# Two transformer blocks on one core: transposed scalar rows made by a round trip through DRAM instead of by TensorE, and two raw weight tiles given up for four more slabs

## The chip, the core and the metric

The kernel runs on one core of a Trainium2 chip. The metric is the device time of one execution in microseconds, the median of several runs. The engines have separate, in-order instruction queues: TensorE (PE, with its weight loads shown as PEld), VectorE (DVE), ScalarE (ACT), GpSimd (POOL) and SyncE (SP, which here issues nearly all DMAs). An instruction that waits holds up everything behind it on its own engine.

## The reference

Input is a sequence of 256 tokens of width 2048. The first block adds, in turn, a mixer, a cross-attention over 256 memory rows and a convolutional feed-forward network; the second block is a hybrid of two attentions. The two places that matter here are these.

In the gated delta rule (8 heads of width 128, chunks of 64) the running sum of the gates makes a matrix of decays for each head:

```
g = jnp.cumsum(g, axis=-1)
decay = jnp.exp(jnp.where(causal, g[..., :, None] - g[..., None, :], -jnp.inf))
a_strict = jnp.where(strict, jnp.einsum('bhncd,bhnmd->bhncm', k_beta, k) * decay, 0.0)
attn = jnp.einsum('bhncd,bhnmd->bhncm', q, k) * decay
```

In the forgetting attention of the second block (8 heads) a running sum over tokens is added to the logits as a bias:

```
c = jnp.cumsum(log_f, axis=1).transpose(0, 2, 1)
logits = jnp.einsum('bhqd,bhsd->bhqs', qb, k, ...) * scale
return logits + cq[:, :, :, None] - c[:, :, None, :]
```

Both need the same small table (128 tokens on partitions by 16 columns: two halves of the sequence, eight heads) in two forms: as a column, one value for each partition, and as a row, the 128 values of one column repeated on all partitions.

## The kernel before, in words

Everything is fp32, computed as products of a high and a low part. All weights are streamed as 704 units of 128 rows by up to 1024 columns (512 KB). For each unit SyncE loads a raw tile (`load`, L365), ScalarE casts it to the high part `whi` (`split_hi`, L372), VectorE subtracts to get the low part `wlo` (`split_lo`, L382) and, as soon as that subtraction is queued, the next load is queued that will reuse this raw tile (`self.load(i + self.NRAW)`: with 8 raw tiles, the load of the unit eight further on). TensorE then multiplies high by high and low (L227), low by high (L231) and for the last block of a job once more (L244). ScalarE is three units ahead of TensorE and VectorE two.

All other work is written as Python generators. `stream` issues one unit, then lets each live generator go to its next `yield`. So a `yield` puts off the rest of a generator by one unit of the stream, about 2.8 us, and the order on each engine is fixed when the program is built.

Intermediate tiles of 128 x 512 floats (2 KB for each partition) come from `S()`, a pool of 55 "slabs"; a new tile takes the slab of a tile that is done, and its first write waits for the last read of that one. A raw tile takes as much as two slabs.

Three stages are touched or spoken of:

- The gates, p_ba (about 40 to 110 us). The running sums land in PSUM and are copied to the table `G` (shown as `keep`, L651). For each of four groups of four heads, `spread` turns four columns to rows: VectorE multiplies a matrix of ones by a column (`dg`, L453, four instructions), TensorE transposes each (L460), and VectorE subtracts the column and takes the negative magnitude (`E`, L665 and L667). The decays are first used at L722.
- The triangular solve, `X`, `Y`, `L` (L765 to L822), runs in four passes from about 170 to 400 us. In a pass, an inverted 16 x 16 base goes out to DRAM (`dA`, `dX`) and back (`X<-dX`, L778). TensorE transposes X into PSUM (L786), ScalarE copies that to `Y` (L789), TensorE multiplies by Y (L797). At the same time `g_mem` (L985 to L1012) reads the memory rows (`mr`) and ScalarE writes their high parts into new slabs (`x`, L1006). `x1` to `x16` are the sixteen tiles of the normalised input, read by the first projections until about 372 us.
- The forgetting attention, fox (about 1860 to 1970 us): `spread` turns two columns for each head, and `fb` (L1385) is the bias.

Of the kernel before, what the change touches and what calls it, by code (L numbers as in the profile page):

```python
# [9 lines left out]
F32 = mybir.dt.float32  # L10
# [6 lines left out]
MUL, ADD, SUB, MAXI, MINI = ALU.mult, ALU.add, ALU.subtract, ALU.max, ALU.min  # L17

P = 128
TOK = 256  # L20
# [79 lines left out]
def r3(ap, n):  # L100
    return ap.rearrange("p (a b) -> p a b", a=n)


def bc(col, n):
    return col.unsqueeze(2).to_broadcast([P, col.shape[1], n])
# [15 lines left out]
class Builder:  # L121
    LOOK_HI = 3
    LOOK_LO = 2
    NRAW = 8

    def __init__(self, ctx, tc, A):
        self.tc, self.nc, self.A = tc, tc.nc, A
# [16 lines left out]
        return pool.tile([P, w], dt, tag=tag, bufs=bufs, name=f"{nm}{self.n}")  # L144

    def S(self, nm, dt=F32):
        return self._t(self.sp, 512, "s", 55, nm, dt)

    def H(self, nm):
        return self._t(self.sp, TOK, "h", 18, nm, F32)  # L150
# [298 lines left out]
    def spread(self, cols, n):  # L449
# [10 lines left out]
            self.T.transpose(ps[:, i * P : (i + 1) * P], w[:, i * P : (i + 1) * P], self.ident)  # L460
        return ps

    def g_rms(self, R, acc, width):

        ps = yield from self.sums([acc])
        yield
        v = self.Cc("v")[:, 0:2]
        self.V.tensor_scalar(v, ps[:, 0:2], 1.0 / width, EPS, MUL, ADD)
        self.psdone()
        R.c = yield from self.rsq(v, 2)  # L470
        ps = yield from self.spread(R.c, 2)
        yield
        R.b = self.H("rb")
        self.AC.copy(R.b, ps[:, 0:TOK])  # L474
        self.psdone()
        R.ok = True
# [134 lines left out]
    def p_ba(self, ps):  # L611
        V, AC = self.V, self.AC
        r = self.H("ba")
        yield from self.times(ps, r, self.r_mix)
        yield
        yield
        while self.psfree < 1:
            yield
        q = self.ps()
        for t in range(2):  # L620
            self.T.transpose(q[:, t * P : (t + 1) * P], r[:, t * P : (t + 1) * P], self.ident)
        yield
        b, z = self.Cc("b"), self.Cc("z")
        b3, z3, q3 = r3(b, 2), r3(z, 2), r3(q[:, 0:TOK], 2)
        V.tensor_copy(b3, q3[:, :, 0:8])
        V.tensor_tensor(z3, q3[:, :, 32:40], bcm(self.col("dtb", 0, 8), 2), ADD)
        self.psdone()
        n, m = self.Cc("n"), self.Cc("m")
        V.scalar_tensor_tensor(n, b, -1.0, b, MUL, MINI)
        V.tensor_scalar(m, b, 0.0, None, MINI)  # L630
        AC.activation(n, n, AF.Exp)
        AC.activation(m, m, AF.Exp)
        ea = self.Cc("ea")[:, 0:8]
        AC.activation(ea, self.col("alog", 0, 8), AF.Exp)
        sp = yield from self.softplus(z, 16)
        V.tensor_scalar(n, n, 1.0, None, ADD)
        V.reciprocal(n, n)
        self.beta = self.gb
        V.tensor_tensor(self.beta, n, m, MUL)
        g = self.Cc("g")  # L640
        V.scalar_tensor_tensor(r3(g, 2), r3(sp, 2), -1.0, bcm(ea, 2), MUL, MUL)
        yield
        yield
        while self.psfree < 1:
            yield
        q = self.ps()
        self.T.matmul(q[:, 0:16], self.upper, g, start=True, stop=True)
        self.T.matmul(q[:, 16:32], self.ones, g, start=True, stop=True)
        yield
        G = self.gG  # L650
        V.tensor_copy(G, q[:, 0:16])  # L651
        ed = self.Cc("ed")
        V.tensor_tensor(ed, q[:, 16:32], G, SUB)
        self.psdone()
        V.tensor_scalar(ed, ed, 0.0, None, MINI)
        AC.activation(self.gE, G, AF.Exp)
        AC.activation(self.gD, ed, AF.Exp)
        self.dec = {}
        for g in range(2):
            for t in range(2):  # L660
                c = G[:, t * 8 + g * 4 : t * 8 + g * 4 + 4]
                q = yield from self.spread(c, 4)
                yield
                e = self.S("E")
                V.tensor_tensor(r3(e, 4), r3(q, 4), bc(c, P), SUB)  # L665
                self.psdone()
                V.scalar_tensor_tensor(e, e, -1.0, e, MUL, MINI)  # L667
                self.dec[g, t] = e
        for e in self.dec.values():
            AC.activation(e, e, AF.Exp)  # L670
        self.gates.ok = True
# [653 lines left out]
    def p_rf(self, ps):  # L1325

        V = self.V
        r = self.H("rf")
        yield from self.times(ps, r, self.rr)
        yield  # L1330
        yield
        while self.psfree < 1:
            yield
        q = self.ps()
        for t in range(2):
            self.T.transpose(q[:, t * P : (t + 1) * P], r[:, t * P : (t + 1) * P], self.ident)
        yield from self.rope(r, self.kr, [self.kr[0:64]])
        self.nc.sync.dma_start(self.kr[64:128], self.kr[0:64])
        self.kr_ev.ok = True
        z = self.Cc("fz")  # L1340
        V.tensor_tensor(r3(z, 2), r3(q[:, 0:TOK], 2)[:, :, 64:72], bcm(self.col("bf", 0, 8), 2), ADD)
        self.psdone()
        V.tensor_scalar(z, z, -1.0, None, MUL)
        sp = yield from self.softplus(z, 16)
        lf = self.Cc("lf")
        V.tensor_scalar(lf, sp, -1.0, None, MUL)
        yield
        while self.psfree < 1:
            yield
        q = self.ps()  # L1350
        self.T.matmul(q[:, 0:8], self.upper, lf[:, 0:8], start=True, stop=True)
        self.T.matmul(q[:, 8:16], self.upper, lf[:, 8:16], start=True, stop=False)
        self.T.matmul(q[:, 8:16], self.ones, lf[:, 0:8], start=False, stop=True)
        yield
        V.tensor_copy(self.cum, q[:, 0:16])
        self.psdone()
        self.cum_ev.ok = True

    def p_qrope(self, j):
# [13 lines left out]
    def g_head(self, score, vals, hcol, out, i, mla):  # L1373
        V, AC, T = self.V, self.AC, self.T
        spans = ((0, 0, P), (1, P, 3 * P))
        bias = None
        if not mla:
            while not (self.cum_ev.ok and self.rr.ok):
                yield
            cols = self.Cc("ck")[:, 0:2]  # L1380
            V.tensor_copy(cols, r3(self.cum, 2)[:, :, i])
            ps = yield from self.spread(cols, 2)
            yield
            bias = self.S("fb")
            V.scalar_tensor_tensor(bias[:, 0:P], ps[:, 0:P], cols[:, 0:1], self.neg[:, 0:P], SUB, ADD)  # L1385
            V.scalar_tensor_tensor(bias[:, P : 3 * P], ps[:, 0:TOK], cols[:, 1:2], self.neg[:, P:], SUB, ADD)
            self.psdone()
        bias = self.neg if bias is None else bias
        while not score.ready():
            yield  # L1390
# [2 lines left out]
        ps = self.ps()  # L1393
# [19 lines left out]
        ps = self.ps()  # L1413
# [9 lines left out]
        ps = self.ps()  # L1423
        c = slice((i % 4) * P, (i % 4 + 1) * P)
# [99 lines left out]
    def build(self):  # L1524
# [54 lines left out]
        first = [mi(32, self.p_ba)] + self.order(gd, zz, sc)  # L1579
        first = self.skew(first, 3, False)  # L1580
# [62 lines left out]
        for si, (a, b) in enumerate(SECTIONS):  # L1643
# [25 lines left out]
            d = self.skew(down, 4)  # L1669
# [64 lines left out]
        gates = [pj(11 + n if n < 8 else 27 + n, self.p_outgate(n)) for n in range(16)]  # L1734

        def fox():
            hs = [self.g_head(self.fox_score(h), self.fvv, 8 + h, self.oat, h, False) for h in range(8)]
            self.add(self.g_chain(hs[0::2]))
            self.add(self.g_chain(hs[1::2]))
# [155 lines left out]
```

## Time and profile before

| | us |
|---|---|
| median of 3 runs | 2075.57 |
| lowest and highest | 2075.34, 2075.96 |
| the profiled execution, device time | 2078.43 |
| span in its trace | 2076.6 |
| TensorE busy in the span | 2054.0 (99%) |
| VectorE, ScalarE, GpSimd busy | 1480.2 (71%), 1088.6 (52%), 158.6 (8%) |

The profiled execution is 2.86 us above the median of the runs; 1.83 us of it lie outside the span. Matmuls are pipelined and their modelled ends overlap the next one's start, so a time from start to start says what one costs on TensorE.

### The profile page before, as it was taken

The page shows a single profiled execution, that of the slowest core. Times are in us where ns is not written, and L with a number is a line of the kernel's source. Part 1 is how long each engine was busy: PE and PEld are TensorE (multiplying, and loading weights), DVE is VectorE, ACT ScalarE, POOL GpSimd, SP SyncE. Part 2 cuts the span into 40 slices and gives each one's busy share as a digit, 9 for nine tenths or more (in the row PEclk, how much of TensorE's full clock was granted, in tenths as well). Part 3 has the DMA queues.
Part 4 walks back from the last instruction along what each step waited for, and adds up shares of the span by engine and source line. Part 5 has one row for each costly group of instructions (what it writes and reads, how often), then busy time and mean ns, then how long its engine had stood idle before and what let it go on. Part 6 is the DMA issues. An engine that isn't in the chain of part 4 may idle for free.

```text
span 2076.6 us, 31002 instructions
## 1 busy us (share of the span) xinstructions
PE 2054.0 (99%) x11730; PEld 1802.1 (87%) x11730; DVE 1480.2 (71%) x2384; ACT 1088.6 (52%) x1736; POOL 158.6 (8%) x149
## 2 busy tenths in 40 slices
PE   9999999899999999999999999999999999999998
PEld 7888898788888898888888888888888888888886
DVE  7988679565467667777875777756879877656755
ACT  6665555444445555455543455434556655445653
POOL 1020011000001001100000000000009420000000
PEclk9999999999999999999999999999999999999999
DMA  8455446446565535556555656555555669544552
GB/s 302 161 184 185 159 155 196 142 152 193 193 223 185 173 119 182 190 187 193 185 193 183 194 189 194 184 191 193 184 168 190 213 216 228 176 160 145 193 192 102
DMA packets 136807, 381.43 MB, mean 184 GB/s; under 512 B 33745, under 2 KB 41681, under 8 KB 136657
## 3 DMA queue, kind: packets, MB, share of 16 engines
q1 hardware_dynamic: 136080, 378.66, 56.6%
q8 instruction: 92, 1.51, 0.3%
q10 hardware_dynamic: 576, 0.79, 0.1%
q14 instruction: 59, 0.48, 0.1%
HBM read 372.85 MB, written 5.90 MB: 182 GB/s over the span
## 4 chain that ended last, share of the span: by engine, by line
PE 92%; DVE 5%; DMA 1%; issue 1%; ACT 1%; POOL 0%; SPq 0%; DVEq 0%; ACTq 0%; POOLq 0%
PE mm L227 46%; PE mm L231 26%; PE mm L326 4%; PE mm L328 4%; PE mm L327 4%; PE mm L244 3%; DVE wlo L382 2%; DMA X<-dX 1%; DVE cv L499 1%; DVE bt L920 0%; PE ps L797 0%; PE ps L432 0%; PE ps L431 0%; PE ps L430 0%; PE ps L1425 0%
## 5 line engine op out<-in xcount | busy, mean ns | idle before, releaser
L227 PE MATMUL mm<-x,whi 128*128 128x512 f32 x4520 | 1120.6, 394 | 1.8 <-DVE x L569 1.2
L227 PEld LDWEIGHTS mm<-x,whi 128*128 128x128 f32 x4520 | 840.4, 189 | 167.6 <-DVE x L569 3.4
L382 DVE TENSOR_TENSOR wlo<-raw,whi 128x1024 fp32r<-128x1024 f32 (+2 forms) x705 | 854.6, 1220 | 181.7 <-ACT whi L372 118.3
L372 ACT CAST whi<-raw 128x1024 fp32r<-128x1024 f32 (+2 forms) x704 | 716.9, 1029 | 269.4 <-PE mm L328 104.4
L231 PEld LDWEIGHTS mm<-x,wlo 128*128 128x128 f32 x4840 | 636.9, 191 | 37.6 <-DVE wlo L382 4.1
L231 PE MATMUL mm<-x,wlo 128*128 128x256 f32 x4840 | 648.3, 283 | 1.9 <-DVE wlo L382 1.9
L249 ACT COPY mg<-mm 128x256 f32<-128x256 f32 x240 | 89.3, 372 | 461.4 <-PE mm L244 460.7
L499 DVE SCALAR_TENSOR_TENSOR cv<-pre,cst,cv 128x256 f32<-128x256 f32 x264 | 129.5, 491 | 70.4 <-ACT cv L496 65.2
L326 PE MATMUL mm<-whi,x 128*128 128x512 f32 x336 | 132.1, 393 | 0.0
L328 PE MATMUL mm<-whi,x 128*128 128x512 f32 x336 | 130.9, 390 | 0.0
L327 PE MATMUL mm<-wlo,x 128*128 128x512 f32 x336 | 130.8, 389 | 0.0
L244 PE MATMUL mm<-x,whi 128*128 128x512 f32 x320 | 126.7, 396 | 0.0
L251 DVE TENSOR_TENSOR ms<-mm,mg 128x256 f32<-128x256 f32 x178 | 74.3, 417 | 20.6 <-ACT mg L249 20.6
L1189 POOL TENSOR_SCALAR hf<-hf,cst 128x256 f32<-128x256 f32 x16 | 25.2, 1575 | 682.2 <-PE mm L244 681.9
L328 PEld LDWEIGHTS mm<-whi,x 128*128 128x128 f32 x336 | 63.1, 188 | 13.3
L327 PEld LDWEIGHTS mm<-wlo,x 128*128 128x128 f32 x336 | 63.1, 188 | 12.9
L326 PEld LDWEIGHTS mm<-whi,x 128*128 128x128 f32 x336 | 63.1, 188 | 12.8
L1171 DVE TENSOR_TENSOR hf<-mm,hf 128x256 f32<-128x256 f32 x48 | 20.2, 421 | 70.8 <-PE mm L244 70.8
L496 ACT ACTIVATE cv<-pre,cst 128x256 f32<-128x256 f32 x120 | 60.5, 506 | 1.9 <-DVE pre L266 1.9
L244 PEld LDWEIGHTS mm<-x,whi 128*128 128x128 f32 x320 | 61.3, 192 | 0.0
L480 ACT ACTIVATE x<-hf,cst 128x256 fp32r<-128x256 f32 x32 | 16.3, 510 | 80.8 <-DVE hf L1066 80.8
L266 DVE TENSOR_TENSOR pre<-ms,rb 128x256 f32<-128x256 f32 x112 | 47.4, 424 | 7.4 <-ACT rb L474 3.9
(342 smaller groups left out, 1206.4 us busy)
## 6 DMA issues: line engine op xcount, KB each, us to landing
raw<-w_ffn_up SPq DMA_DIRECT2D x176, 512.0 KB, 3.8
raw<-w_mix_in SPq DMA_DIRECT2D x114, 512.0 KB, 3.8
raw<-w_in SPq DMA_DIRECT2D x86, 512.0 KB, 3.5
raw<-w_ffn_down SPq DMA_DIRECT2D x80, 512.0 KB, 3.4
raw<-w_xk SPq DMA_DIRECT2D x32, 512.0 KB, 3.7
raw<-w_xv SPq DMA_DIRECT2D x32, 512.0 KB, 3.3
raw<-w_mix_out SPq DMA_DIRECT2D x32, 512.0 KB, 3.2
raw<-w_xq SPq DMA_DIRECT2D x32, 512.0 KB, 3.3
```

The source lines that it names most:

```text
L227: self.T.matmul(ps, hi[:, (j0 + j) * P : (j0 + j + 1) * P], x.t, start=first and j == 0, stop=False)
L231: self.T.matmul(ps[:, 0:TOK], lo[:, (j0 + j) * P : (j0 + j + 1) * P], xs[k0 + j].hi, start=False, stop=False)
L244: self.T.matmul(ps, hi[:, (j0 + m) * P : (j0 + m + 1) * P], xs[k0 + m].t, start=first and m == 0, stop=True)
L249: self.AC.copy(t, ps[:, TOK:])
L251: self.V.tensor_tensor(out, ps[:, 0:TOK], t, ADD)
L326: self.T.matmul(ps, x.hi[:, s], hi[:, c], start=k == 0, stop=False)
L327: self.T.matmul(ps, x.hi[:, s], lo[:, c], start=False, stop=False)
L328: self.T.matmul(ps, x.lo[:, s], hi[:, c], start=False, stop=k == K - 1)
L372: self.nc.scalar.copy(hi[:, 0:F], self.raw[i][:, 0:F])
L382: self.nc.vector.tensor_tensor(lo[:, c[0] : c[1]], r[:, c[0] : c[1]], h[:, c[0] : c[1]], SUB)
L496: self.AC.activation(t, pre[:, o : o + TOK], AF.Identity, scale=taps[:, 0:1])
L499: self.V.scalar_tensor_tensor(t, pre[:, o + j : o + j + TOK], taps[:, j : j + 1], t, MUL, ADD)
```

## The change

`spread` is no longer called in the two stages. A table goes to DRAM in transposed form with one DMA on GpSimd's queue (`rows_out`: the source is 128 partitions of 16 values, the destination 16 rows of 128, so neighbouring values of a partition lie 512 bytes apart), and each group of rows is read back with a step of zero over the partitions (`rows_in`: 128 x 4 pieces of 512 bytes for a gate group, 128 x 2 for a head of fox). The four gate groups are asked for right after the table, one for each unit; three yields follow, then the arithmetic. Fox asks for a head's row two heads ahead. Raw tiles go from 8 to 6 and slabs from 55 to 59, which takes the same memory.

```diff
-    NRAW = 8
+    NRAW = 6
...
-        return self._t(self.sp, 512, "s", 55, nm, dt)
+        return self._t(self.sp, 512, "s", 59, nm, dt)
...
+    def rows_out(self, cols, name):
+
+        d = self.dp.tile([16, P], F32, name=name)
+        self.G.dma_start(bass.AP(tensor=d.tensor, offset=0, ap=[[1, P], [P, 16]]), cols)
+        return d
+
+    def rows_in(self, d, first, step, n):
+
+        w = self.S("dr")
+        src = bass.AP(tensor=d.tensor, offset=first * P, ap=[[0, P], [step * P, n], [1, P]])
+        self.G.dma_start(r3(w[:, 0 : n * P], n), src)
+        return w
...
-        self.dec = {}
+        self.dec, rows = {}, {}
+        d = self.rows_out(G, "dG")
+        yield
+        for g in range(2):
+            for t in range(2):
+                yield
+                rows[g, t] = self.rows_in(d, t * 8 + g * 4, 1, 4)
+        yield
+        yield
+        yield
         for g in range(2):
             for t in range(2):
                 c = G[:, t * 8 + g * 4 : t * 8 + g * 4 + 4]
-                q = yield from self.spread(c, 4)
-                yield
-                e = self.S("E")
-                V.tensor_tensor(r3(e, 4), r3(q, 4), bc(c, P), SUB)
-                self.psdone()
+                e = rows.pop((g, t))
+                V.tensor_tensor(r3(e, 4), r3(e, 4), bc(c, P), SUB)
+                yield
                 V.scalar_tensor_tensor(e, e, -1.0, e, MUL, MINI)
...
+        self.cum_d = self.rows_out(self.cum, "dC")
         self.cum_ev.ok = True
...
-            ps = yield from self.spread(cols, 2)
+            row = self.rows.pop(i)
+            if i + 2 < 8:
+                self.rows[i + 2] = self.rows_in(self.cum_d, i + 2, 8, 2)
             yield
             bias = self.S("fb")
-            V.scalar_tensor_tensor(bias[:, 0:P], ps[:, 0:P], cols[:, 0:1], self.neg[:, 0:P], SUB, ADD)
-            V.scalar_tensor_tensor(bias[:, P : 3 * P], ps[:, 0:TOK], cols[:, 1:2], self.neg[:, P:], SUB, ADD)
-            self.psdone()
+            V.scalar_tensor_tensor(bias[:, 0:P], row[:, 0:P], cols[:, 0:1], self.neg[:, 0:P], SUB, ADD)
+            V.scalar_tensor_tensor(bias[:, P : 3 * P], row[:, 0:TOK], cols[:, 1:2], self.neg[:, P:], SUB, ADD)
...
         def fox():
+            self.rows = {i: self.rows_in(self.cum_d, i, 8, 2) for i in range(2)}
```

Line numbers of the changed program are 13 to 20 higher in these stages. GpSimd in the gates, before (`r` is the inverse norm, `kq` a masked product of the delta rule):

```order
L526 MEMSET neg 128x128
L591 ISA
L591 TENSOR_TENSOR r_554<-rb_551 128x256
L726 TENSOR_TENSOR kq_1321<-kq_1321,mats 128x512
L726 TENSOR_TENSOR kq_1325<-kq_1325,mats 128x512
L761 TENSOR_TENSOR kd_1534<-ktm_1402,keep 128x512
```

and in the changed program, in the same place:

```order
L539 MEMSET neg 128x128
L604 ISA
L604 TENSOR_TENSOR r_550<-rb_547 128x256
L466 DMA dG<-keep 128x16x1
L473 DMA dr_898<-dG 128x512
L473 DMA dr_929<-dG 128x512
L473 DMA dr_963<-dG 128x512
L473 DMA dr_991<-dG 128x512
L746 TENSOR_TENSOR kq_1283<-kq_1283,mats 128x512
L746 TENSOR_TENSOR kq_1287<-kq_1287,mats 128x512
```

The write of the table and the four reads now stand between `r` and `kq`; the first read waits for the write to land, and nothing else stands between.

VectorE in the gates, before, from the copy of the table on:

```order
L651 COPY keep<-ps_794 128x16
L653 TENSOR_TENSOR ed_831<-ps_794,keep 128x16
L655 TENSOR_SCALAR ed_831<-ed_831 128x16
L453 TENSOR_SCALAR dg_836<-mats,keep 128x128 x4
L499 SCALAR_TENSOR_TENSOR cv_770<-pre_80,cst,cv_770 128x256 x3
L266 TENSOR_TENSOR pre_82<-ms_760,rb_551 128x256
L382 TENSOR_TENSOR wlo_851<-raw_561,whi_805 128x1024
L499 SCALAR_TENSOR_TENSOR cv_803<-pre_81,cst,cv_803 128x256 x3
```

and in the changed program where the first two rows are used (L685 and L687 are what L665 and L667 were; `cv`, `ms` and `pre` belong to the projections):

```order
L512 SCALAR_TENSOR_TENSOR cv_998<-pre_81,cst,cv_998 128x256 x3
L251 TENSOR_TENSOR ms_1021<-mm_974,mg_1022 128x256
L266 TENSOR_TENSOR pre_82<-ms_1021,rb_547 128x256
L382 TENSOR_TENSOR wlo_1057<-raw_877,whi_1026 128x1024
L685 TENSOR_TENSOR dr_898<-dr_898,keep 128x512
L382 TENSOR_TENSOR wlo_1087<-raw_910,whi_1055 128x1024
L687 SCALAR_TENSOR_TENSOR dr_898<-dr_898 128x512
L685 TENSOR_TENSOR dr_929<-dr_929,keep 128x512
```

The four `dg` instructions behind the table are gone. The first use of a row now stands eight `wlo` behind L668 (which was L655), and between other `wlo`; the later rows follow one unit apart. On TensorE four groups of four transposes go here, and four groups of four in fox.

ScalarE at about 360 to 379 us, before, with the numbers of the tiles and the semaphores that each instruction waits for (PE_49 is TensorE's):

```order
L249 COPY mg819_3962<-mm813_3917 128x256 [waits PE_49]
L1006 ACTIVATE x820_3964<-mr783_3782,cst_74 128x256 [waits PE_49]
L496 ACTIVATE cv814_3936<-pre2_81,cst_74 128x256 [waits Pool_49]
L372 CAST whi821_3967<-raw780_3759 128x1024 [waits DMAHW6_49,DVE_49]
L978 CAST x827_4004<-scb803_3897 128x256 [waits DVE_49,PE_49]
L372 CAST whi828_4007<-raw787_3792 128x1024 [waits DMAHW0_49,Activation_49]
L249 COPY mg832_4030<-mm824_3973 128x256
L789 COPY Y833_4032<-ps825_3990 128x512 [waits PE_49]
L789 COPY Y834_4034<-ps826_3995 128x512 [waits PE_49]
```

and in the changed program:

```order
L249 COPY mg809_3924<-mm803_3879 128x256 [waits PE_49]
L1026 ACTIVATE x810_3926<-mr773_3744,cst_74 128x256
L509 ACTIVATE cv804_3898<-pre2_81,cst_74 128x256 [waits Pool_49]
L372 CAST whi811_3929<-raw782_3785 128x1024 [waits DMAHW7_49,DVE_49]
L998 CAST x817_3966<-scb793_3859 128x256 [waits DVE_49]
L372 CAST whi818_3969<-raw788_3815 128x1024 [waits DMAHW2_49,PE_49,Activation_49]
L249 COPY mg822_3992<-mm814_3935 128x256 [waits PE_49]
L809 COPY Y823_3994<-ps815_3952 128x512
L809 COPY Y824_3996<-ps816_3957 128x512
```

The same instructions stand in the same order. Slabs are handed out otherwise: `x820` before is written into the slab of `x1`, the first tile of the input, and so waits for TensorE; `x810`, its counterpart, takes the slab of a read memory row and has no wait of its own. The slab of `x1` now goes to `x826`, behind the two copies to `Y`.

## Rows read from the trace of the kernel before

**Rows 1.** Page, part 1: busy us (share), instructions of each engine
```profile
PE 2054.0 (99%) x11730; PEld 1802.1 (87%) x11730; DVE 1480.2 (71%) x2384; ACT 1088.6 (52%) x1736; POOL 158.6 (8%) x149
```

**Rows 2.** Chain of waits, 60 to 110 us: start us, us, what
```profile
82.18 0.79 DVE dg L453 x4
...
85.11 1.23 DVE wlo L382
...
93.42 0.44 PE ps L460 x4
```

**Rows 3.** Timeline, TensorE, 82 to 89 us: start us, us, instructions [idle before <-releaser]
```profile
82.99 0.60 PE L460 MATMUL ps<-mats,dg 128*128 128x128 f32 x4
...
86.38 1.22 PE L231 MATMUL mm<-x,wlo 128*128 128x256 f32 x8 [1.17 <-DVE wlo L382]
```

**Rows 4.** Timeline, ScalarE, 356 to 383 us
```profile
360.08 0.37 ACT L249 COPY mg<-mm 128x256 f32<-128x256 f32 x1 [1.54 <-PE mm L244]
372.15 0.51 ACT L1006 ACTIVATE x<-mr,cst 128x256 fp32r<-128x256 f32 x1 [11.70 <-PE mm L231]
...
376.54 0.40 ACT L978 CAST x<-scb 128x256 fp32r<-128x256 f32 x1 [2.54 <-DVE scb L976]
...
378.06 1.08 ACT L789 COPY Y<-ps 128x512 f32<-128x512 f32 x2
...
379.54 0.52 ACT L1006 ACTIVATE x<-mr,cst 128x256 fp32r<-128x256 f32 x1
```

**Rows 5.** Timeline, TensorE, 180 to 384 us
```profile
187.04 1.95 PE L797 MATMUL ps<-Y,L 128*128 128x128 f32 x16
...
364.31 0.66 PE L786 MATMUL ps<-mats,X 128*128 128x128 f32 x4 [1.48 <-DMA X<-dX]
...
369.77 0.40 PE L244 MATMUL mm<-x,whi 128*128 128x512 f32 x1
...
378.79 3.75 PE L797 MATMUL ps<-Y,L 128*128 128x128 f32 x16 [5.84 <-ACT Y L789]
```

**Rows 6.** Windows: busy us of each engine (instructions), granted clock, DMA share, GB/s
```profile
365.50:368.92 3.42, 3.42 (x11) 2.74 (x10) 0.00 (x0) 0.00 (x0) 0.00 (x0) 0.50 0.53 217
...
375.74:382.57 6.83, 3.78 (x17) 3.81 (x18) 6.05 (x11) 5.40 (x9) 0.45 (x1) 0.50 0.53 162
```

**Rows 7.** Timeline, VectorE, 66 to 116 us
```profile
70.64 0.17 DVE L651 COPY keep<-ps 128x16 f32<-128x16 f32 x1
...
80.76 0.68 DVE L665 TENSOR_TENSOR E<-ps,keep 128x512 f32<-128x512 f32 x1
...
96.23 2.35 DVE L382 TENSOR_TENSOR wlo<-raw,whi 128x1024 fp32r<-128x1024 f32 x2
...
113.31 0.68 DVE L722 TENSOR_TENSOR A<-ps,E 128x512 f32<-128x512 f32 x1
```

**Rows 8.** Timeline, GpSimd, 0 to 130 us
```profile
46.52 0.85 POOL L591 TENSOR_TENSOR r<-rb 128x256 f32<-128x256 f32 x1 [23.16 <-ACT rb L474]
114.67 3.53 POOL L726 TENSOR_TENSOR kq<-kq,mats 128x512 f32<-128x512 f32 x2 [67.30 <-DVE kq L723]
```

**Rows 9.** DMA issues: queue, count, KB each, median us from issue to landing
```profile
raw<-w_mix_in SPq DMA_DIRECT2D x114, 512.0 KB, 3.8
...
X<-dX SPq DMA_DIRECT2D x4, 256.0 KB, 6.7
...
dX<-bw SPq DMA_DIRECT2D x4, 32.0 KB, 3.8
```

**Rows 10.** Source line L453: durations ns min/median/max, first and last start
```profile
L453 DVE TENSOR_SCALAR dg<-mats,ck x16: 279/284/290, 1860.7 to 1959.8; 128x128 f32<-128x128 f32 x16
```

**Rows 11.** Waits: us in total, times, longest us
```profile
POOL sw L1319 <- DMA sw<-qr: 76.6, 4, 60.0
```

**Rows 12.** Timeline, SyncE queue, 1591 to 1606 us
```profile
1595.36 9.78 SPq L365 DMA_DIRECT2D raw<-w_in  x6
```

**Rows 13.** Timeline, ScalarE, 1591 to 1606 us
```profile
1602.75 1.55 ACT L372 CAST whi<-raw 128x512 fp32r<-128x512 f32 x2
```

## Prediction

> **What bounds the kernel now.** The page comes first: TensorE is busy 99% of the span, VectorE 71%, GpSimd 8% [rows 1]. So there are two ways to gain: fewer or faster instructions on TensorE, or an end to one of its few waits. Work taken from another engine counts only where TensorE waits for that engine. The chain of waits then says where that is. From 66 to 86 us VectorE carries the chain, through two groups of `dg` to a `wlo` that starts at 85.11 [rows 2], and TensorE's timeline shows the price: 1.17 us idle before 86.38, released by VectorE [rows 3]. Soon after it TensorE carries the chain again, the transposes among the rest.
>
> The third place is the largest, and ScalarE's timeline is to be read for it. At 360.45 a copy ends, and ScalarE sits idle 11.70 us, until TensorE has done an L231; what waits is the high part of a memory row, L1006 [rows 4]. It has no data from TensorE: it waits for its slab, the one of `x1`. Behind it in ScalarE's queue stand the two copies to `Y`, at 378.06. TensorE's timeline [rows 5] shows what that does: L797 needs `Y`, TensorE is through with all ahead of it at 378.79 - 5.84 = 372.95, and waits 5.84 us. Then its 16 matmuls take 3.75 us, where an undisturbed group took 1.95. The windows say why: the granted clock was 0.50 from 375.74 to 382.57 [rows 6], 1.2 in place of 2.4 GHz, and TensorE had stood still before the clock fell. There is a similar piece at 365.50 [rows 6], behind a wait of 1.48 us for `X<-dX` [rows 5].
>
> **What the change removes.** Eight groups of four transposes go, four in the gates and four in fox. In the chain a group counts 0.44 us [rows 2]; on the timeline four last 0.60 us, the overlap with the next matmul included [rows 3]. I take 0.53, about midway, since the next matmul also starts slower behind a change of shape: 8 x 0.53 = 4.2 us, with 3.5 and 4.8 as bounds. These lie on TensorE, the bound, so they come off in full.
>
> On VectorE 32 `dg` go. In fox TensorE waits hardly at all, so that is worth nothing there. In the gates two groups of 0.79 us and one pair of L665 and L667, 0.68 us for the first of them [rows 2, 7], stood on VectorE ahead of 85.11 and no longer do: over 2.2 us against a wait of 1.17. I put the wait at nothing left, 1.2 us gained; the bounds are 0 and 1.2.
>
> **What the four slabs do.** The order shows that the L1006 of 372.15 no longer waits for TensorE, since `x1`'s slab goes to the next one (379.54 before [rows 4]), which stands behind the copies to `Y`. So ScalarE goes on at 360.45. From that L1006 to the copies it took 378.06 - 372.15 = 5.9 us, a wait of 2.54 for VectorE included [rows 4]; from 360.45 that is 366.4. The last thing to wait for is the `mg` copy ahead of `Y`, which needs the L244 that starts at 369.77 [rows 5] and ends by 370.2. That copy (0.37) and two to `Y` (1.08) make 371.6, which is 1.3 us before TensorE comes. So the wait of 5.84 us goes, and with it the half clock on L797, 3.75 - 1.95 = 1.80 us: 7.6 us. Bounds: 0, if the cure moves the wait to another slab; 7.6. The wait of 1.48 us at 364.31 ends with a DMA on SyncE, whose place among the loads does not move, so I leave it. Late next is then the `mg` copy.
>
> **What it adds.** On GpSimd five DMAs between `r`, which ends at 47.4, and `kq` at 114.67; GpSimd is idle in between for 67.30 us [rows 8], so nothing queued behind them is held up. The table is ready at 70.64 + 0.17 = 70.8 [rows 7]. The first use stands eight `wlo` later; counting them in the old timeline leads to the first of the pair at 96.23, which ends at 97.4 [rows 7]. Less what TensorE no longer loses, that is about 95. So 24 us are there for: the table out, landed, the first row in. The trace has no DMA from GpSimd's queue and none with 4-byte pieces. The nearest rows are a write of 512 pieces of 64 bytes, `dX<-bw`, with 3.8 us to landing, and a read of 512 pieces of 512 bytes, `X<-dX`, with 6.7 us, the size of a row group (pieces by their patterns) [rows 9]. Lower bound: 3.8 + 6.7 = 10.5 us. With four times the pieces at four times the time, the table takes 4 x 3.8 = 15.2, the chain 21.9: still in time. Upper bound: four times 6.7 for the table as well, 33.5 us, which is 9 us late. I take a value between the first two, so no wait, because a landing has a fixed part that doesn't grow with the pieces.
>
> The Trainium skill, "DMA: Bandwidth & Descriptors", section "Rules for kernel authors", speaks against this write: with a strided last dimension there is one descriptor for each element, here 2048. The same page, section "Anatomy of one DMA — SWDGE (gpsimd) path", gives about 2.0 us plus bytes over 436 GB/s for a DMA from GpSimd and says many descriptors can be emitted before that shows; by it table and first row take an estimated 4.6 us, and the sum stays. No row here shows either.
>
> In fox the two rows of a head are asked for two heads ahead; `ck`'s `dg` for eight heads run from 1860.7 to 1959.8 in pairs [rows 10], so two heads are some 33 us, and the reads are hidden even at 33 us. Behind the table of fox GpSimd later waits 60.0 us for another DMA [rows 11], which covers its write. Worth nothing. If that cover were gone, each late head would cost what it is late.
>
> Six raw tiles: a load still goes out behind a `wlo`, but serves the unit six ahead. The tightest place I found outside the start: a `wlo` frees a tile and the loads go out at 1595.36 [rows 12]; the cast of the unit six on stands in the pair at 1602.75 [rows 13]. 7.4 us, less 3.8 to landing [rows 9], leave 3.6; even a landing of 6.7 would leave 0.7. Worth nothing; if the cover went, each such unit would cost its lateness.
>
> **Sum.** 4.2 + 1.2 + 7.6 = 13.0 us. The profiled execution would go from 2078.43 to 2065.4; it lies 2.86 above the median of the runs, so the median goes from 2075.57 to 2062.6.
>
> **Rivals.**
> 1. The slabs move the wait rather than end it: another tile in front of `Y` meets a late reader. For it: with a pool in rotation every tile's slab changes. Against: in the order, neither that L1006 nor the copies to `Y` wait for TensorE by themselves. Then 4.2 + 1.2 = 5.4 are left: 2070.2.
> 2. The first row is late by up to 9 us (the upper bound). VectorE works in order, so the `wlo` behind the subtraction are late, and TensorE has about one unit, 2.8 us, in hand. A loss of 3 to 6 us: 2066 to 2069.
> 3. The rows come one after another, each with its own 6.7 us behind a table of 26.8: the last lands at 70.8 + 26.8 + 4 x 6.7 = 124.4, where it is wanted at about 103. VectorE is then 21 us late and TensorE 18 or so; the gain of 1.2 is lost too. 2075.57 - 11.8 + 18 = 2082: slower. It decides from a last row at about 118 on.
> 4. `X<-dX` comes in time as well, as fewer loads are under way: 1.48 us more, and 1.7 of half clock (the 3.42 us of work in the window at 365.50 would be 1.71): 2062.6 - 3.2 = 2059.4.
> 5. Six tiles starve some casts, at a few us in all: 2064 to 2072.
>
> The Trainium skill, "SBUF — State Buffer", in its box on DVE blocking a DMA, would favour 2 and 3: GpSimd writes the descriptors and is shut out while VectorE runs a two-port operation such as `tensor_scalar`. The change itself takes the large `tensor_scalar` out of this stage; what is left beside the wait are mostly operations with two inputs, which the page doesn't count. By it the rows would be late only behind small ones, and the sum stays. No run here shows it yet.
>
> **Chances.** Forecast 0.62; rival 1 0.12; 2 0.10; 3 0.05; 4 0.06; 5 0.05. A change of under 0.2%, 4.15 us, can't be told from none. Faster by more (under 2071.4): the forecast, rivals 2 and 4, and somewhat under half of 1 and 5, which lie near that bound: 0.62 + 0.10 + 0.06 + 0.07 = 0.85. Within: most of what 1 and 5 leave, 0.09. Slower: rival 3 and 0.01 of 5: 0.06. The range goes from 2058, below rival 4 by a little, to 2071, above 1 and 2.
>
> **What would show it.** In the changed profile: 16 L460 instead of 48; no L1006 on ScalarE that waits for TensorE at 360 us, L797 without a wait there and at 1.95 us, and one half-clock window fewer; no wait of VectorE for `dr` at 95 us; no casts that wait for loads. Wrong it goes if VectorE waits for `dr`, or if ScalarE waits for a slab in front of `Y` once more.

## The result and the profile after

The changed kernel takes 2062.65 us (median of 4 runs, 2062.38 to 2063.18) against 2075.77 (4 runs, 2075.34 to 2075.97): a ratio of 0.9936, 95% interval 0.9920 to 0.9952, or 13.1 us less. The forecast was 2062.6, 13.0 us less. Not every term of that sum was right, though, and two errors cancelled.

The page of the changed kernel, part 1, beside [rows 1]: TensorE is busy 7.7 us less and the span is 15.5 us shorter (2076.6 before).

```profile
span 2061.1 us, 30928 instructions
...
PE 2046.3 (99%) x11698; PEld 1795.9 (87%) x11698; DVE 1470.9 (71%) x2352; ACT 1088.2 (53%) x1736; POOL 169.1 (8%) x163
```

ScalarE's timeline of the changed kernel, where [rows 4] had the idle time of 11.70 us:

```profile
356.12 0.37 ACT L249 COPY mg<-mm 128x256 f32<-128x256 f32 x1 [1.55 <-PE mm L244]
356.39 0.51 ACT L1026 ACTIVATE x<-mr,cst 128x256 fp32r<-128x256 f32 x1
...
362.89 0.37 ACT L249 COPY mg<-mm 128x256 f32<-128x256 f32 x1 [1.20 <-PE mm L244]
363.16 1.08 ACT L809 COPY Y<-ps 128x512 f32<-128x512 f32 x2
```

The high part of the memory row (L1026, L1006 before) follows the `mg` copy at once. The copies to `Y` wait only for the `mg` copy ahead of them, as forecast, and end at 364.24 (363.16 + 1.08). TensorE's timeline, which answers to [rows 5]:

```profile
358.71 1.36 PE L806 MATMUL ps<-mats,X 128*128 128x128 f32 x8
...
362.69 2.00 PE L227 MATMUL mm<-x,whi 128*128 128x512 f32 x8
364.53 1.11 PE L231 MATMUL mm<-x,wlo 128*128 128x256 f32 x8
365.48 1.95 PE L817 MATMUL ps<-Y,L 128*128 128x128 f32 x16
```

L817 (L797 before) follows the L231 without a wait and takes the 1.95 us of an undisturbed group. L806 doesn't wait for `X<-dX` either, 1.48 us before.

Three views follow: GpSimd's timeline, with the new DMAs in the time that was idle in [rows 8]; VectorE's timeline at the first use of a row; and the table's line of the DMA issues (KB, us from issue to landing).

```profile
46.45 0.85 POOL L604 TENSOR_TENSOR r<-rb 128x256 f32<-128x256 f32 x1 [23.11 <-ACT rb L487]
71.05 1.34 POOL L466 DMA_DIRECT2D dG<-keep  x1 [23.75 <-DVE ed L666]
83.07 2.18 POOL L473 DMA_DIRECT2D dr<-dG  x4 [10.68 <-DMA dG<-keep]
111.30 3.53 POOL L746 TENSOR_TENSOR kq<-kq,mats 128x512 f32<-128x512 f32 x2 [26.06 <-DVE kq L743]
```

```profile
92.29 0.68 DVE L685 TENSOR_TENSOR dr<-dr,keep 128x512 f32<-128x512 f32 x1
```

```profile
dG<-keep POOLq DMA_DIRECT2D x1, 8.0 KB, 11.7
```

The table took 11.7 us to landing. The first row was asked for at 83.07 and took the least of the four, 7.4 us (the other three up to 10.5), so it was there at 90.45, and it is used at 92.29 without a wait. The chain took 19.4 us, between the two values of the prediction that were in time (10.5 and 21.9), and 1.8 us were left (1.3 in `after_again` below, the same kernel profiled once more).

To see where the time went, the start of the same TensorE instruction was compared in two traces, and the difference taken between places of the program. I did this for the first pair of profiles and for a second pair, `before_again` and `after_again` below (times of before; us by which the changed kernel gains):

```
stretch                                   first pair  second pair  forecast
to 70                                         0.06        0.30        -
gates, 70 to 110                              3.31        3.31       3.3 (2.1 transposes + 1.2 wait)
110 to 350                                    0.60       -0.38        -
350 to 370: X<-dX and the clock after it      3.34        1.31        0
370 to 383: Y, and the clock after it         7.88        7.60       7.6
383 to 1860                                   0.01        0.05        0
fox, 1860 to the end                          0.45        0.46       2.1
```

The gates and the slab are where they were put. Fox gave a fifth of its term, and `X<-dX`, which the sum had left alone, gave something in its place.

What one group of transposes cost can be read from start to start. TensorE's timeline of the kernel before, in the gates:

```profile
93.25 0.60 PE L460 MATMUL ps<-mats,dg 128*128 128x128 f32 x4
93.61 2.10 PE L227 MATMUL mm<-x,whi 128*128 128x512 f32 x8
95.55 1.11 PE L231 MATMUL mm<-x,wlo 128*128 128x256 f32 x8
```

From 93.25 to 95.55 are 2.30 us. Eight L227 without transposes take 1.84 (362.69 to 364.53 above), so by these rows the group costs 0.46 us, a slower first matmul behind it included. Counted matmul by matmul in the trace it is 0.44 for each of the eight groups. So each stage is rid of 1.8 us of transposes, and the other 1.5 us of the gates are nearly all the wait for VectorE and a slower start behind it.

### The profile page after: what moved, and what is told of

It is laid out like the page before. It is cut to its first block, busy times and chain, and to the rows that moved or that the text cites. A ratio compares the mean times of both kernels' runs of the same rounds, so it can differ in the third digit from the quotient of the medians.

```text
span 2061.1 us, 30928 instructions
## 1 busy us (share of the span) xinstructions
PE 2046.3 (99%) x11698; PEld 1795.9 (87%) x11698; DVE 1470.9 (71%) x2352; ACT 1088.2 (53%) x1736; POOL 169.1 (8%) x163
## 4 chain that ended last, share of the span: by engine, by line
PE 96%; DVE 2%; DMA 1%; ACT 1%; issue 0%; POOL 0%; SPq 0%; DVEq 0%; ACTq 0%; POOLq 0%
PE mm L227 48%; PE mm L231 27%; PE mm L326 4%; PE mm L328 4%; PE mm L327 4%; PE mm L244 4%; DVE wlo L382 1%; PE ps L431 0%; PE ps L432 0%; PE ps L430 0%; PE ps L817 0%; PE ps L1447 0%; DMA X<-dX 0%; PE ps L806 0%; PE ps L834 0%
## 5 line engine op out<-in xcount | busy, mean ns | idle before, releaser
L227 PE MATMUL mm<-x,whi 128*128 128x512 f32 x4520 | 1118.9, 393 | 1.8 <-DVE x L582 1.2
L227 PEld LDWEIGHTS mm<-x,whi 128*128 128x128 f32 x4520 | 839.5, 188 | 167.3 <-DVE x L582 3.1
L231 PEld LDWEIGHTS mm<-x,wlo 128*128 128x128 f32 x4840 | 636.8, 191 | 35.7 <-DVE wlo L382 2.2
L231 PE MATMUL mm<-x,wlo 128*128 128x256 f32 x4840 | 648.0, 283 | 0.6 <-DVE wlo L382 0.6
```

Of the source, the lines that this page charges most:

```text
L227: self.T.matmul(ps, hi[:, (j0 + j) * P : (j0 + j + 1) * P], x.t, start=first and j == 0, stop=False)
L231: self.T.matmul(ps[:, 0:TOK], lo[:, (j0 + j) * P : (j0 + j + 1) * P], xs[k0 + j].hi, start=False, stop=False)
```

## Experiments

### Slabs and rows apart

`slabs_only`: the kernel before with the two numbers of the change alone.

```diff
-    NRAW = 8
+    NRAW = 6
...
-        return self._t(self.sp, 512, "s", 55, nm, dt)
+        return self._t(self.sp, 512, "s", 59, nm, dt)
```

> The kernel before with 6 raw tiles and 59 slabs; rows still come from TensorE. In its order the L1006 ahead of the two copies to Y has no wait for TensorE. Theory: the slab of the first input tile was the whole of the largest term, 5.8 us of waiting and 1.8 to 2.0 us of half clock, and six raw tiles cost nothing: 7.6 to 7.9 us less than before, about 2068, and L797 does not wait near 370 us. Rival: the wait moves to another tile or the smaller number of raw tiles costs: 2071 to 2076.

2066.71 us, ratio 0.9958 (0.9946 to 0.9970), against 2075.39 for before on that chip: 8.7 us less. That is more than the 7.6 to 7.9 expected, but the interval (6.2 to 11.2 us) includes them. L797 has no wait:

```profile
370.77 1.95 PE L797 MATMUL ps<-Y,L 128*128 128x128 f32 x16
```

`rows_only`: the changed kernel with the two numbers put back.

```diff
-    NRAW = 6
+    NRAW = 8
...
-        return self._t(self.sp, 512, "s", 59, nm, dt)
+        return self._t(self.sp, 512, "s", 55, nm, dt)
```

> The changed kernel with 8 raw tiles and 55 slabs, so only the rows through DRAM. In its order the L1026 ahead of the copies to Y waits for TensorE as before. Theory: the wait of about 5.8 us at L817 near 370 us stays with its half clock; the gates give 3.3 us (four groups of transposes at 0.5 and a wait of 1.3), fox about 0.5: 3.5 to 5.5 us less than before, 2070.3 to 2072.3. Rival: the rows themselves free the chain ahead of Y: 2063 to 2066.

2070.92 us, ratio 0.9977 (0.9968 to 0.9986): 4.5 us less. The wait is there still, and so is the half clock (3.76 us for 16 matmuls):

```profile
370.99 3.76 PE L817 MATMUL ps<-Y,L 128*128 128x128 f32 x16 [5.84 <-ACT Y L809]
```

The two parts add up: 8.7 + 4.5 = 13.2. Two thirds of the gain of a change about rows came from two numbers that make room for them.

`two_slabs`: the kernel before with one raw tile given up for two slabs.

```diff
-    NRAW = 8
+    NRAW = 7
...
-        return self._t(self.sp, 512, "s", 55, nm, dt)
+        return self._t(self.sp, 512, "s", 57, nm, dt)
```

> The kernel before with 7 raw tiles and 57 slabs: two slabs more instead of four. Now the slab of the first input tile goes to the second of the two copies to Y itself, so that a wait for TensorE still stands in front of L797, but with nothing between: the copy takes 0.5 us from the release, and TensorE itself needs 0.8 us from there to L797. Theory (what costs is the work queued between the waiting instruction and Y, not the wait): L797 waits under 0.3 us, and the time is that of 59 slabs, 2066 to 2068.5. Rival (any reuse of that slab ahead of L797 costs): a wait of several us and half clock, 2070 to 2075.

2067.87 us, ratio 0.9962 (0.9948 to 0.9976), 7.0 us less than the 2074.91 of before on that chip. ScalarE's timeline shows that a wait for TensorE is still there, on the second copy itself:

```profile
367.77 0.59 ACT L789 COPY Y<-ps 128x512 f32<-128x512 f32 x1
369.46 0.59 ACT L789 COPY Y<-ps 128x512 f32<-128x512 f32 x1 [1.09 <-PE mm L231]
```

TensorE showed no wait at L797 all the same:

```profile
370.10 1.95 PE L797 MATMUL ps<-Y,L 128*128 128x128 f32 x16
```

So it was not the reuse of that slab that cost, but the five instructions between the one that waited and `Y`, with a wait for VectorE among them.

`raw6_only`: the kernel before with `NRAW = 6` alone.

> The kernel before with 6 raw tiles and still 55 slabs, so less memory used. Theory: six raw tiles cost nothing: 2074.5 to 2076.5. Rival: casts that wait for loads cost 1 us or more, hidden in the gain of the slabs: 2076.5 to 2079.

2075.29 us against 2074.91, ratio 1.0001 (0.9991 to 1.0010): no cost. L797 waits its 5.84 us as before.

`five_raw`: the changed kernel with `NRAW = 5`.

> The changed kernel with 5 raw tiles: a load goes out one unit later again, about 2.8 us. By the tightest place read from the trace of before (3.6 us in hand with six) 0.8 us are left outside the gates; in the gates casts waited 7.8 us in six places with six tiles, which will be about 2.8 us more at each. Theory: VectorE and TensorE have two units in hand, so the time is within 1 us of the changed kernel, 2062 to 2064. Rival: the slack is used up and TensorE waits: 2065 to 2075.

2062.65 us, ratio 0.9938 (0.9923 to 0.9953), level with the changed kernel. Casts do wait longer for their loads; the waits by engine, in us in all, times and longest, first of the changed kernel, then of this one:

```profile
ACT whi L372 <- DMA raw<-w_mix_in: 7.8, 6, 2.1
```

```profile
ACT whi L372 <- DMA raw<-w_mix_in: 9.3, 8, 3.1
...
ACT whi L372 <- DMA raw<-w_uq: 6.4, 4, 2.4
```

The change is far less than the 2.8 us more at each place that were expected. Three of the six waits lie ahead of 20 us, where the kernel before has three as well (3.1 us). None of it shows in the time.

### Fox

`gates_only`: the changed kernel with fox as before.

```diff
-            row = self.rows.pop(i)
-            if i + 2 < 8:
-                self.rows[i + 2] = self.rows_in(self.cum_d, i + 2, 8, 2)
+            ps = yield from self.spread(cols, 2)
             yield
...
-        self.cum_d = self.rows_out(self.cum, "dC")
...
-            self.rows = {i: self.rows_in(self.cum_d, i, 8, 2) for i in range(2)}
```

> The changed kernel with the fox stage as before (rows of the forget biases by TensorE). Forecast before the result: fox is worth 2.1 us, so this would be 2064.7. By the two traces aligned instruction by instruction fox gave only 0.5 us, since the shorter chain now makes TensorE wait 0.9 us for VectorE at the transposes of the softmax (L1437): then this is 2063.0 to 2063.4, within half a microsecond of the changed kernel.

2063.80 us, ratio 0.9942 (0.9929 to 0.9954), above the 2063.0 to 2063.4 expected. The medians put fox at about 1 us, across two chips; the alignment of this trace with that of `after_again` below puts it at 0.46 between two places ahead of and behind fox, the rest of the difference being elsewhere. Either is well short of 2.1. TensorE's timeline of `after_again` has the new wait, none of which stood in fox before:

```profile
1887.48 2.00 PE L227 MATMUL mm<-x,whi 128*128 128x512 f32 x8
1890.08 0.61 PE L1437 MATMUL ps<-mats,lg 128*128 128x128 f32 x3 [0.60 <-DVE lg L1431]
1890.95 0.61 PE L1437 MATMUL ps<-mats,lg 128*128 128x128 f32 x3 [0.27 <-DVE lg L1431]
1891.32 1.87 PE L227 MATMUL mm<-x,whi 128*128 128x512 f32 x7
```

`spread` held two yields; without them the softmax of two heads reaches its transposes before VectorE is done. The idle times in brackets, 0.87 us, count from the modelled ends of the matmuls. From start to start the wait costs more. The eight L227 would be through at 1889.32, 1.84 us after their start; the first transpose starts 0.76 later. The six then take 1.24 us to the next matmul at 1891.32, where six undisturbed take 0.57 (1866.83 to 1867.40 below). That is 1.4 us lost, against the 1.8 us that the transposes of `spread` had cost here. It leaves about 0.4, near the 0.46 measured.

`fox_extra` gives one unit back, behind the softmax; `after_again` is the changed kernel beside it.

```diff
             V.tensor_scalar(lg[:, a:b], lg[:, a:b], sm[:, t : t + 1], None, MUL)
         yield
+        if not mla:
+            yield
```

> The changed kernel with one more yield ahead of the transposes of the softmax in fox. Theory: the new wait of TensorE at L1437 (0.9 us idle, 1.2 us in all near 1890 us) comes from a chain that became shorter; with one unit more it is gone and the kernel is 0.8 to 1.3 us faster than the changed one. Rival: the wait turns up at the next step of the chain: within 0.3 us of it.

> The changed kernel once more, for comparison on one chip with the kernels beside it: 2062.0 to 2063.5. X<-dX lands within 5.0 to 6.0 us of its issue again and L806 near 358 us waits under 0.3 us, as in the first profile, if the shorter landing belongs to the change and not to that execution.

`fox_extra` took 2062.30 us (2061.42 to 2062.78, 5 runs), ratio 0.9934 (0.9922 to 0.9947); `after_again` 2062.93 (2062.26 to 2063.94), ratio 0.9938 (0.9926 to 0.9951). It is the lowest median of the study, but not told apart from the changed kernel. TensorE's timeline marks no wait any more, but two of the groups take longer than an undisturbed one:

```profile
1866.83 0.82 PE L1439 MATMUL ps<-mats,lg 128*128 128x128 f32 x6
1867.40 3.70 PE L227 MATMUL mm<-x,whi 128*128 128x512 f32 x15
...
1892.45 2.00 PE L227 MATMUL mm<-x,whi 128*128 128x512 f32 x8
1894.50 1.27 PE L1439 MATMUL ps<-mats,lg 128*128 128x128 f32 x6
1895.52 1.87 PE L227 MATMUL mm<-x,whi 128*128 128x512 f32 x7
...
1951.97 1.27 PE L1439 MATMUL ps<-mats,lg 128*128 128x128 f32 x6
```

VectorE's timeline at the first of the two:

```profile
1894.07 0.55 DVE L1431 TENSOR_SCALAR lg<-lg,sm 128x128 f32<-128x128 f32 x2
...
1894.72 0.55 DVE L1431 TENSOR_SCALAR lg<-lg,sm 128x128 f32<-128x128 f32 x2
```

The six at 1894.50 start 0.2 us after the L227 ahead of them are through, and take 1.02 us to the next matmul in place of 0.57. In the trace the first transpose of each head starts 0.15 us, and the second 0.06, behind the end of the L1431 instruction that makes its data. So TensorE still waits for VectorE, in pieces too short for the timeline to mark. At 0.66 us each the two places cost 1.3 us, against the 1.4 of the one wait in the changed kernel, and between the same two places of the program TensorE gains only 0.2 us over `after_again`. The theory of 0.8 to 1.3 us was too much. The gain in the trace is within the rival's 0.3 us, though the wait did not go to the next step: it stands at the same step, a shorter one at the same two heads and another at the last two. A kernel with both units given back was not run.

### The rows' way

`early_use` moves the three yields behind the arithmetic; only instructions of VectorE change their place (eight of them in the trace, not the six of the expectation).

```diff
-        yield
-        yield
-        yield
         for g in range(2):
...
                 self.dec[g, t] = e
+        yield
+        yield
+        yield
```

> The changed kernel with the three yields behind the requests moved behind the arithmetic: six instructions of VectorE stand three units earlier, nothing else moves on any engine. The first use then stands where VectorE was at 84.4 us in the changed kernel, and the first row landed at 90.45 us there. Theory (rival 2 of the prediction, with one unit in hand): VectorE waits 6.0 us for the row, the low parts behind it are late, TensorE loses 6.0 - 2.8 = 3.2 us, up to 5 with half clock after it: 2065.5 to 2068. Rival: TensorE has two low parts in hand and loses nothing: 2062.3 to 2063.3. Other rival: nothing in hand, all 6 us lost and half clock after: 2069 or more.

2070.53 us, ratio 0.9976 (0.9965 to 0.9986): 7.6 us more than `after_again` on that chip. VectorE's timeline, then TensorE's, then two windows:

```profile
90.42 0.69 DVE L682 TENSOR_TENSOR dr<-dr,keep 128x512 f32<-128x512 f32 x1 [6.51 <-DMA dr<-dG]
```

```profile
94.53 2.08 PE L231 MATMUL mm<-x,wlo 128*128 128x256 f32 x8 [5.28 <-DVE wlo L382]
...
96.83 3.16 PE L227 MATMUL mm<-x,whi 128*128 128x512 f32 x8
```

```profile
92.00:96.00 4.00, 1.47 (x7) 1.47 (x8) 3.93 (x8) 2.81 (x4) 0.00 (x0) 0.56 0.42 150
96.00:100.00 4.00, 4.00 (x14) 3.26 (x14) 3.90 (x8) 0.79 (x2) 0.00 (x0) 0.58 0.64 235
```

VectorE waits 6.51 us, of which TensorE loses 5.28, and in that standstill the granted clock falls (0.56 and 0.58 in the two windows). Eight L227 behind it take 3.16 us in place of 2.00. The other rival of the expectation held: little more than a microsecond is in hand in this stage, and the half clock comes on top.

`rows_on_sync` has SyncE issue the same DMAs.

```diff
-        self.G.dma_start(bass.AP(tensor=d.tensor, offset=0, ap=[[1, P], [P, 16]]), cols)
+        self.nc.sync.dma_start(bass.AP(tensor=d.tensor, offset=0, ap=[[1, P], [P, 16]]), cols)
...
-        self.G.dma_start(r3(w[:, 0 : n * P], n), src)
+        self.nc.sync.dma_start(r3(w[:, 0 : n * P], n), src)
```

> The changed kernel with the table writes and row reads issued by SyncE, in the same places of the program. On GpSimd's queue the table took 11.7 us from issue to landing and the first row 7.4. Theory A: the 2048 pieces of 4 bytes take the time, whoever issues them: 9 to 12 us on SyncE too. Theory B: GpSimd's queue takes it: 4 to 6 us on SyncE. In either case the first read now holds up the loads behind it until the table has landed; with 6 raw tiles and about 10 us in hand that costs TensorE nothing under B (2062 to 2064) and 0 to 6 us under A (2062 to 2069).

2062.72 us, ratio 0.9937 (0.9923 to 0.9950). The table again took 11.7 us, so the time isn't that of GpSimd's queue (theory A), and the loads held up behind it cost nothing. The timeline of SyncE's queue shows the hold, and the DMA packets of 71 to 83 us show the pieces, 2080 packets under 512 bytes where the kernel before has 48:

```profile
70.74 0.43 SPq L466 DMA_DIRECT2D dG<-keep  x1
73.76 3.69 SPq L365 DMA_DIRECT2D raw<-w_mix_in  x2
82.46 0.33 SPq L473 DMA_DIRECT2D dr<-dG  x1
```

```profile
DMA packets 2277, 0.82 MB, mean 68 GB/s; under 512 B 2080, under 2 KB 2080, under 8 KB 2277
```

### The wait for X<-dX

`before_again`: the kernel before, unchanged.

> The kernel before, unchanged, profiled once more. Between the two profiled executions TensorE lost 3.2 us less around 364 to 369 us (the wait for X<-dX and the half clock after it), which the forecast had left in place, yet the medians moved by the forecast 13.1 us. Theory A: that wait belongs to the one profiled execution of before, which was 2.86 us above its median. Then L786 waits under 0.5 us near 364 us here, there is one half-clock stretch fewer, and the span is about 2073.7 us. Theory B: every execution of before has it, and the change removed it: then the wait of about 1.5 us is here again and the span is 2076.6 us.

One run of 2074.86 us, span 2073.1. Both theories hold in part:

```profile
362.54 0.66 PE L786 MATMUL ps<-mats,X 128*128 128x128 f32 x4 [1.04 <-DMA X<-dX]
```

```profile
364.00:368.00 4.00, 4.00 (x23) 3.44 (x22) 0.00 (x0) 0.00 (x0) 0.00 (x0) 1.00 0.50 202
```

The wait is there again, with 1.04 us, but no half clock behind it (1.00 in the window). `slabs_only` waited longer and has none either:

```profile
363.85 0.66 PE L786 MATMUL ps<-mats,X 128*128 128x128 f32 x4 [1.37 <-DMA X<-dX]
```

So that half clock, some 1.7 us, was in the one execution profiled at first and in none of the other profiles; it would account for more than half of the 2.86 us by which that one stood above its median. (The 1.83 us outside its span are no part of that: here 1.8 us lie outside the span too.) The wait is in both. In `after_again` `X<-dX` took 5.3 and 5.7 us, and L806 waited 0.15, as expected if the shorter landing belongs to the change.

`spare_table`: the kernel before with an unused table in DRAM.

```diff
             self.nc.sync.dma_start(block_rows(self.dX[t]), r3(zero, 4))
+        spare = self.dp.tile([16, P], F32, name="dG")
+        self.nc.sync.dma_start(bass.AP(tensor=spare.tensor, offset=0, ap=[[16, P], [1, 16]]), zero[:, 0:16])
```

> The kernel before with one more table of 8 KB in DRAM, written once with zeros at the start and never read. X<-dX in the second group took 6.6 to 7.4 us to landing in every profile without the gate rows and 5.2 to 5.8 us in those with them, though the loads around it are the same. Theory: the place of the tiles in DRAM makes the difference: 5.2 to 5.8 us here, and L786 waits under 0.3 us. Rival: it hangs on what the gates' rows do to the rest: 6.6 to 7.4 us and a wait of 1.0 to 1.5 us.

Neither theory: 5.7 and 6.3 us to landing, and a wait of 0.48 us (one run, 2075.20 us).

```profile
362.84 0.66 PE L786 MATMUL ps<-mats,X 128*128 128x128 f32 x4 [0.48 <-DMA X<-dX]
```

Over all profiles, the two `X<-dX` at about 353 to 361 us took 5.0 to 6.5 us in the eight with the gates' rows and 5.7 to 7.4 in the six without: they overlap, so a difference by chance is not excluded, and why the landing varies stays open.

## Why the prediction was right, step by step

- The transposes: forecast 8 x 0.53 = 4.2 us, measured 0.44 for a group in both stages, 3.5 in all. The mechanism is right, the size 0.7 too much; the 0.44 of the chain was the right reading.
- The wait of 1.17 us for VectorE in the gates went in full. With the slower start behind it that gave 1.5 us rather than 1.2.
- The slabs: forecast 7.6, traces 7.88 and 7.60; shown by `slabs_only` and `rows_only`, with the mechanism by `two_slabs`. The copies to `Y` ended 1.2 us before TensorE came (364.24 and 365.48), where 1.3 was forecast. Rival 1, that the wait only moves, was wrong: with 59 slabs no copy to `Y` waits for a slab, and with 57 the wait did move, and cost nothing.
- Fox, the mis-sized term: forecast 2.1, measured 0.46. The step that failed was "these lie on TensorE, the bound, so they come off in full". The transposes came off, 1.8 us, but the change also shortens the chain of a head by the two yields of `spread`, which the prediction did not weigh for fox. TensorE then lost 1.4 us at the transposes of the softmax, waiting for VectorE. `fox_extra` shows that giving one unit back only spreads that wait over two places (1.3 us); that both units would end it is argued and not shown.
- `X<-dX` was left out of the sum (rival 4, 0.06). TensorE did lose 1.3 to 1.6 us less there in the two pairs, the clock aside, though not because fewer loads are under way: `rows_only` with its eight raw tiles had it as short. This made up for most of fox, and without it the forecast would have been more than 1 us off. That the sum came within 0.1 us is luck to that extent.
- The rows' way: in time, as forecast, with 19.4 us of 21 rather than the 24 counted. The first use came at 92.3 and not at 95, since VectorE got further ahead of TensorE. The table alone took 11.7 us; scaling by pieces had given 15.2. The estimate of 2.0 us from the Trainium skill ("DMA: Bandwidth & Descriptors", "Anatomy of one DMA — SWDGE (gpsimd) path") is far off here, and the measurement decides. The trace agrees with the rule of the Trainium skill ("DMA: Bandwidth & Descriptors", "Rules for kernel authors") that a strided last dimension means one descriptor for each element: 2080 small packets for 2048 values in `rows_on_sync`, and 8 KB in 11.7 us, where 32 KB in 64-byte pieces took 3.8.
- The price of rival 2 was wrong. "About one unit in hand" would have made 6.5 us of waiting cost 3.7; `early_use` lost 7.6. The kernel stood 1.8 us from this, 1.3 in `after_again`.
- The Trainium skill ("SBUF — State Buffer", the box on DVE blocking a DMA in "SBUF: two separate sides") advises to issue from another queue a DMA that VectorE holds up on GpSimd's. Here that would not have helped: `rows_on_sync` took as long for the table and in all. Only the rows came sooner, the first 5.2 us after its issue in place of 7.4, and nothing waited for them.
- Six raw tiles cost nothing, as forecast (`raw6_only`), and five cost nothing either (`five_raw`).
- Of the signs, "no casts that wait for loads" did not come: three casts waited behind the table in the gates (the last section). The others did. There are two half-clock stretches fewer rather than one, since the one behind `X<-dX` was of one execution.

## What to carry to other kernels

Where buffers come from one rotating pool, ask of each wait on a queue what the waiting instruction needs: if it is only its place, then two buffers more or fewer can be worth more than the change that they belong to, and what counts is what stands behind it. A step that is taken off an engine's path also takes its yields off a chain; look at what now comes too early. Read the price of a wait from start to start: the idle time that a timeline marks can be less (0.87 us marked in fox, 1.4 lost), and short waits are not marked at all. Prices of late data should be worked out with the clock after the standstill, not only with what is in hand.

## What the hardware showed that I had not expected

The transposed table holds up the weight loads. Windows of the changed kernel while it is under way (the last columns are the share of the DMA engines' time and GB/s), then of the kernel before:

```profile
74.00:77.00 3.00, 3.00 (x19) 2.62 (x18) 2.90 (x7) 3.00 (x7) 0.00 (x0) 1.00 0.10 1
77.00:80.00 3.00, 3.00 (x19) 2.62 (x18) 2.93 (x6) 2.14 (x4) 0.00 (x0) 1.00 0.48 41
80.00:83.00 3.00, 3.00 (x19) 2.62 (x18) 2.90 (x7) 1.68 (x5) 0.00 (x0) 1.00 0.53 34
```

```profile
74.00:77.00 3.00, 3.00 (x19) 2.58 (x19) 2.89 (x6) 2.80 (x6) 0.00 (x0) 1.00 0.36 113
77.00:80.00 3.00, 3.00 (x21) 2.70 (x20) 2.93 (x6) 1.71 (x3) 0.00 (x0) 1.00 0.37 111
80.00:83.00 3.00, 3.00 (x20) 2.63 (x19) 2.96 (x8) 1.37 (x3) 0.00 (x0) 1.00 0.69 243
```

For some 9 us the core moves 1 to 41 GB/s in place of 111 to 243, and a raw load issued at 74.09 landed only at 85.77, 11.7 us later, where the median of these loads on the profile's page is 4.2. With SyncE as the issuer the load behind the table took 11.5. At the 113 GB/s of the first window a table of 8 KB thus holds up an estimated 1 MB of other transfers. TensorE lost nothing by it here; it is busy for all of the three windows. With eight raw tiles no cast waits for a load behind the table (`rows_only`, where all three such waits lie ahead of 20 us). With six, three casts do, 4.8 us in all in the changed kernel, the first of them at the late load:

```profile
85.87 1.06 ACT L372 CAST whi<-raw 128x1024 fp32r<-128x1024 f32 x1 [2.14 <-DMA raw<-w_mix_in]
```

ScalarE was far enough ahead for that. So six raw tiles, which cost nothing by themselves, have less to spare once the table is there.

It seems to be the pieces and not the 8 KB. The unused table of `spare_table` has as many bytes, written in 64-byte pieces from SyncE at 26.06 us. It took 7.1 us to landing, among loads that took 5.9 to 7.5, and held up nothing: 408 GB/s in this window, 404 in the kernel before.

```profile
26.00:29.00 3.00, 3.00 (x19) 2.63 (x18) 2.96 (x5) 2.06 (x4) 0.00 (x0) 1.00 1.02 408
```

That stage is another one, though, and in the gates a table laid out otherwise wasn't tried.
